# Thirteen accumulating transfers begun by GpSimd beside four pairs of gate and up units of a decoder layer

## The chip, the cores and the metric

The kernel runs on one core of a Trainium2 chip. A core has TensorE (matrix products), VectorE, ScalarE and GpSimd (called POOL in the profile), and SyncE (SP), whose queue begins most transfers; sixteen transfer engines move the bytes. Each engine works through its instructions in order. The metric is the time of one execution on the device in microseconds; smaller is better. A profiled execution has a span as well, from its first to its last instruction.

## The reference

One decoder layer on 2048 tokens of width 1024: a mixing block of two head groups (a gated linear recurrence, and sliding-window attention with sinks), an output projection, and a gated MLP with a causal convolution of three taps; then a normalisation. The change lies in the MLP, which is

```python
v = rmsnorm(h, norm_ffn_w[l])
gate = causal_depthwise_conv(v @ w_gate[l], conv_w[l], conv_b[l])
h = h + (jax.nn.silu(gate) * (v @ w_up[l])) @ w_down[l]
```

with D_FF = 2816 columns in w_gate and w_up.

## The kernel before, in words

Activations lie transposed: features on the 128 partitions, tokens along the row. The tokens are worked in two halves (hf = 0 and 1) of 1024. In each half come the mixing block, the output projection, the stage gate_up, and the stage down. All operands are fp32 split into a high and a low part, and each product of blocks is three matmuls.

gate_up loops over 11 pairs (pr = 0 to 10) of feature tiles, 2 x 128 columns of w_gate and of w_up. A pair is two units, one for gate and one for up. A unit is a 2 x 2 block product done with seven block products in place of eight (Winograd's form): on the weight side the blocks are A11, A12, A22 and the sums S1 to S4, on the token side B11, B21, B22 and T1 to T4. Its 84 matmuls of 512 columns go to three banks X, Z and Y; ScalarE copies the results s1, u2, s5 and u3 to a ring of seven tiles of 128 x 512 (tag "ut", UT = 7), and VectorE adds them up.

prep_pair loads the two weight tiles of the next unit (raw4 at L192, on SP's queue, into a ring of three raw tiles), forms S1 to S4 on VectorE (L934 to L937), and splits all operands: the high part is a cast on ScalarE (L800), the low part a subtraction on VectorE (L801).

After the gate unit follow convolution, SiLU and the normalising factor, which give two tiles y1 and y2 of 128 x 1024; the evacuation of the up unit multiplies its results into them (L1085), half by half. They come from a pool of eight tiles of 128 x 1024 (slot, tag "m"), which also holds S, Sh, Sl and S4 of the weights. At the end of a pair the seven token-side operands of the down stage are formed and stored to scratch in device memory:

```python
nc.sync.dma_start(dst["B11"], y1[:, lo])      # L1095; B21 and B22 from y2 follow
...
nc.vector.tensor_tensor(y1[:, lo], tt[:, hi], y1[:, lo], op=ALU.add)       # L1102
nc.sync.dma_start(dst["T2"], y1[:, lo])                                    # L1103
nc.vector.tensor_tensor(y2[:, lo], y2[:, lo], y1[:, lo], op=ALU.subtract)  # L1104
nc.sync.dma_start(dst["T4"], y2[:, lo])                                    # L1105
```

So the lower halves of y1 and y2 are overwritten in place, and whatever reads them must have read them before. These operands (act0B11, act0T4 and so on) are read again only in the down stage, whose products are written out in `product` and `prep_piece`.

The framework derives all waits from the reads and writes of tiles, and plans the order of each engine's instructions ahead of time with estimated times of its own (`schedule_with_timeline_sim=True`); the text's order is only a priority, except where `issue_after` pins it. GpSimd works in the head of the kernel and sets zeros in the mixing block; in gate_up it has nothing to do, and it begins no transfer anywhere.

Of the kernel before, what the change touches and what calls it, by code (L numbers as in the profile page):

```python
# [8 lines left out]
F32 = mybir.dt.float32  # L9
# [4 lines left out]
ALU = mybir.AluOpType  # L14
# [3 lines left out]
P = 128  # L18
D = 1024
# [21 lines left out]
UT = 7  # L41
# [12 lines left out]
def hymba_layer(ctx: ExitStack, tc: tile.TileContext, a: dict, out: bass.AP):  # L54
    nc = tc.nc

    def pool(name, bufs=1, space=None, stack=ctx, **kw):
        if space is not None:
            kw["space"] = space
        return stack.enter_context(tc.tile_pool(name=name, bufs=bufs, **kw))  # L60
# [7 lines left out]
    dp = pool("dram", space=bass.MemoryType.DRAM)  # L68
# [277 lines left out]
    def slot(name):  # L346
        return hp.tile([P, HALF], F32, tag="m", name=name, bufs=KT)
# [455 lines left out]
    @contextmanager  # L803
    def behind(*instructions):

        with ExitStack() as st:
            for i in instructions:
                st.enter_context(tc.issue_after(i.ins))
            yield
# [102 lines left out]
    def prep_pair(src1, src2, home=None, ut=None):  # L912

        r1, r2 = raw4(src1), raw4(src2)
        lo, hi = slice(0, 512), slice(512, D)

        def ring():
            return (wp.tile([P, D], F32R, tag="hi", name="whi", bufs=2),
                    wp.tile([P, D], F32R, tag="lo", name="wlo", bufs=2))

        def m(name, shape=[P, D], dt=F32R):
            return hp.tile(shape, dt, tag="m", name=name, bufs=KT)

        A = None if home else ring()
        if A:
            split_into(*A, r1)

        if home:
            S1, S2, S4 = [ut(n) for n in ("S1", "S2", "S4")]
        else:  # L930
            S = m("S", [P, D], F32)
            S1, S2, S4 = S[:, lo], S[:, hi], r1[:, hi]
        B = Sh, Sl = [(home or m)(n) for n in ("Sh", "Sl")]
        nc.vector.tensor_tensor(S1, r2[:, lo], r2[:, hi], op=ALU.add)  # L934
        nc.vector.tensor_tensor(S2, S1, r1[:, lo], op=ALU.subtract)
        nc.vector.tensor_tensor(r2[:, lo], r1[:, lo], r2[:, lo], op=ALU.subtract)
        nc.vector.tensor_tensor(S4, r1[:, hi], S2, op=ALU.subtract)  # L937
        if home:
            split_into(Sh[:, hi], Sl[:, hi], S2)
            split_into(Sh[:, lo], Sl[:, lo], S1)  # L940
        else:
            split_into(Sh, Sl, S)
        if not A:
            A = ring()
            split_into(*A, r1)
        R = ring()
        dd = m("S4", [P, 2, 512])

        def rest():
            split_into(*R, r2)  # L950
            split_into(dd[:, 0], dd[:, 1], S4)

        if not home:
            rest()
        cut = lambda t, c: (t[0][:, c], t[1][:, c])
        return {"A11": cut(A, lo), "A12": cut(A, hi), "S1": cut(B, lo), "S2": cut(B, hi),
                "S3": cut(R, lo), "A22": cut(R, hi), "S4": (dd[:, 0], dd[:, 1]), "rest": rest}
# [65 lines left out]
    def gate_up(hf, ops, hs, nxt, last, p):  # L1023

        acts = {op: [dp.tile([P, n, 512], F32, name=f"act{hf}{op}{i}") for i, n in enumerate(PIECES)] for op in OPS}
        lo, hi = slice(0, 512), slice(512, HALF)
        invb = hs.acc

        def ring(name, dt=F32):
            return p.tile([P, 512], dt, tag="ut", name=name, bufs=UT)  # L1030

        srcs = [w[2 * pr:2 * pr + 2] for pr in range(FT // 2) for w in (a["w_gate"], a["w_up"])]
        for pr in range(FT // 2):
            f0 = 2 * pr
            W, nxt = nxt, None

            ga = [p.tile([P, HALF + 64], F32, tag="ga", name="ga", bufs=2)[:, 0:2 + HALF] for _ in range(2)]

            def gate(i, j, x, y):
                dst = ga[i][:, 2 + j * 512:2 + (j + 1) * 512]  # L1040
                iv = invb[:, j * 512:(j + 1) * 512]
                if y is not None:
                    nc.vector.tensor_tensor(dst, x, y, op=ALU.add)
                    x = dst
                later.append(lambda: nc.vector.tensor_tensor(dst, x, iv, op=ALU.mult))
                if pr:
                    flush()

            def flush():
                while later:  # L1050
                    later.pop(0)()

            later = []
            then = {"S4": lambda: hs.everywhere(ring, ("mm", "mm"), True), "A22": flush} if pr == 0 else {}
            if pr == 0:
                def behind_first(copied):
                    nonlocal nxt
                    with behind(*last(copied)):
                        nxt = prep_pair(srcs[1][0], srcs[1][1])

                pair_unit(W, ops, p, gate, then, behind_first)
            else:
                nxt = prep_pair(srcs[2 * pr + 1][0], srcs[2 * pr + 1][1])
                pair_unit(W, ops, p, gate, then)
            flush()
            ys = []
            for i in range(2):
                ft, g = f0 + i, ga[i]
                nc.scalar.copy(g[:, 0:2], halo[:, ft])
                nc.scalar.copy(halo[:, ft], g[:, HALF:HALF + 2])  # L1070
                y = slot("y")
                nc.scalar.activation(y, g[:, 2:2 + HALF], AF.Identity, scale=C.cw[:, ft, 2:3], bias=C.cw[:, ft, 3:4])  # L1072
                for w in (1, 0):
                    nc.vector.scalar_tensor_tensor(y, g[:, w:w + HALF], C.cw[:, ft, w:w + 1], y,  # L1074
                                                   op0=ALU.mult, op1=ALU.add)
                nc.scalar.activation(y, y, AF.Silu)
                nc.vector.tensor_tensor(y, y, invb, op=ALU.mult)
                ys.append(y)

            def up(i, j, x, y):  # L1080
                dst = ys[i][:, j * 512:(j + 1) * 512]
                if y is not None:
                    nc.vector.tensor_tensor(y, x, y, op=ALU.add)
                    x = y
                nc.vector.tensor_tensor(dst, x, dst, op=ALU.mult)  # L1085

            W = nxt
            if pr + 1 < FT // 2:
                nxt = prep_pair(srcs[2 * pr + 2][0], srcs[2 * pr + 2][1])
            pair_unit(W, ops, p, up)  # L1090

            y1, y2 = ys
            dst = {op: acts[op][pr // 2][:, pr % 2] for op in OPS}
            tt = slot("T13")
            nc.sync.dma_start(dst["B11"], y1[:, lo])  # L1095
            nc.sync.dma_start(dst["B21"], y2[:, lo])
            nc.sync.dma_start(dst["B22"], y2[:, hi])
            nc.vector.tensor_tensor(tt[:, lo], y1[:, hi], y1[:, lo], op=ALU.subtract)
            nc.sync.dma_start(dst["T1"], tt[:, lo])
            nc.vector.tensor_tensor(tt[:, hi], y2[:, hi], y1[:, hi], op=ALU.subtract)  # L1100
            nc.sync.dma_start(dst["T3"], tt[:, hi])
# [4 lines that stand above are left out]
        return acts  # L1106
# [184 lines left out]
    for hf in range(NH):  # L1291
        X, kv, invb, rs, f0 = nxt
        with ExitStack() as st:
            p = pool(f"mix{hf}", stack=st, reuse_waits="tile")
# [7 lines left out]
            for n, step in enumerate(ORDER.split()):  # L1302
                i = int(step[1:] or 0)
# [16 lines left out]
        with ExitStack() as st:  # L1320
            p = pool(f"ffn{hf}", stack=st, reuse_waits="tile")
            kept, ops, hs, first, last = out_proj(hf, M, p)
            acts = gate_up(hf, ops, hs, first, last, p)
            nxt = down(hf, kept, acts, p)
# [61 lines left out]
```

## Time and profile before

| | |
|---|---|
| time, median of 2 runs | 2113.93 us (2113.62 to 2114.24) |
| span of the profiled execution | 2112.5 us |
| the profiled execution's own time | not listed apart from the runs; their median is 1.4 us above the span |
| TensorE matmul, busy | 2098.0 us (99%) |
| VectorE / ScalarE / GpSimd, busy | 1624.3 / 1088.1 / 24.6 us |
| SP's and ScalarE's hardware queues | 251.45 and 1.85 MB |
| mean granted clock of TensorE | 0.999 |

The page gives busy times by engine for the whole span, and shares of time of the chain of work that ended last; other views of the same trace give the instructions in order of time (start, duration, engine, line, operation, output and inputs, and in brackets the idle time before with what ended it), the waits summed by pairs of lines (total, number, longest), and busy times in chosen stretches. A busy TensorE counts overlapping matmuls once. "SPq" rows are SP's issues of transfers: their duration is that of the issue and not of the transfer.

### The profile page before, as it was taken

Reading aid. Unit: us, or ns where it says so; the run is one execution under the profiler, and the core shown is the slowest. Engines: PE = TensorE matmul, PEld = TensorE weight load, DVE = VectorE, ACT = ScalarE, POOL = GpSimd, SP = SyncE. Lnnn points to the kernel's source line nnn. Section 1 sums busy time; section 2 is a strip of 40 time slices with the busy share of each in tenths; the row PEclk is TensorE's granted clock in tenths of the full one; section 3 lists DMA queues with packets and bytes.
Section 4 is the critical chain, followed back from the end, with each engine's and each line's share of the span. In section 5 each row is a group of like instructions: output and inputs, shape, how many; then the busy total and the mean of one; then the engine's idle time right before and its main releaser. Section 6 shows DMA issues by size and latency. Waiting matters only on the chain.

```text
span 2112.5 us, 29613 instructions
## 1 busy us (share of the span) xinstructions
PE 2098.0 (99%) x11480; PEld 1740.9 (82%) x11480; DVE 1624.3 (77%) x2355; ACT 1088.1 (52%) x1877; POOL 24.6 (1%) x52
## 2 busy tenths in 40 slices
PE   9999999999999999999999999999999999999998
PEld 7888888888888888888888888888888888888887
DVE  7457887898888878786773677868988788887766
ACT  6365565664444445345744566656544444444354
POOL 2000000000000000000000000000000000000000
PEclk9999999999999999999999999999999999999999
DMA  4111111513332325964641111214233233269643
GB/s 161 42 51 34 33 42 53 175 60 115 102 122 86 119 96 185 389 213 157 218 134 52 31 34 35 77 45 149 80 100 130 88 102 120 85 217 385 230 149 135
DMA packets 96617, 255.19 MB, mean 121 GB/s; under 512 B 17370, under 2 KB 19802, under 8 KB 96476
## 3 DMA queue, kind: packets, MB, share of 16 engines
q1 hardware_dynamic: 91220, 251.45, 34.9%
q10 hardware_dynamic: 5256, 1.85, 0.3%
q8 instruction: 90, 1.47, 0.3%
q14 instruction: 51, 0.42, 0.1%
HBM read 195.11 MB, written 57.16 MB: 119 GB/s over the span
## 4 chain that ended last, share of the span: by engine, by line
PE 96%; ACT 2%; DMA 1%; DVE 1%; issue 0%; SPq 0%; DVEq 0%
PE X L975 8%; PE X L976 8%; PE X L977 8%; PE pop L222 7%; PE hq L222 4%; PE q L222 4%; PE f L222 4%; PE pdx L1193 4%; PE pdx L1194 4%; PE pdx L1195 4%; PE Y L977 4%; PE Y L976 4%; PE Y L975 4%; PE g L222 3%; PE pdy L1194 3%; PE pdy L1193 3%
## 5 line engine op out<-in xcount | busy, mean ns | idle before, releaser
L800 ACT CAST whi<-raw 128x1024 fp32r<-128x1024 f32 x88 | 92.6, 1052 | 110.0 <-PE X L976 74.1
L975 PE MATMUL X<-T,whi 128*128 128x512 f32 x352 | 137.4, 390 | 0.0
L976 PE MATMUL X<-T,whi 128*128 128x512 f32 x352 | 137.0, 389 | 0.0
L977 PE MATMUL X<-T,wlo 128*128 128x512 f32 x352 | 137.0, 389 | 0.0
L1074 DVE SCALAR_TENSOR_TENSOR y<-ga,cw,y 128x1024 f32<-128x1024 f32 x88 | 112.3, 1278 | 25.7 <-ACT y L1072 25.7
L201 DVE TENSOR_TENSOR wlo<-raw,whi 128x1024 fp32r<-128x1024 f32 x57 | 69.3, 1218 | 60.8 <-ACT whi L200 60.5
L982 ACT COPY u<-X 128x512 f32<-128x512 f32 x88 | 51.6, 587 | 121.4 <-PE X L977 121.3
L801 DVE TENSOR_TENSOR wlo<-raw,whi 128x1024 fp32r<-128x1024 f32 x88 | 107.1, 1217 | 2.1 <-ACT whi L800 2.1
L200 ACT CAST whi<-raw 128x1024 fp32r<-128x1024 f32 x57 | 59.6, 1048 | 77.9 <-PE q L222 22.3
L222 PE MATMUL pop<-XL,whi 128*128 128x512 f32 x256 | 88.8, 391 | 0.0
L222 PE MATMUL pop<-XH,whi 128*128 128x512 f32 x256 | 88.0, 393 | 0.0
L222 PE MATMUL pop<-XH,wlo 128*128 128x512 f32 x256 | 87.1, 390 | 0.0
L801 DVE TENSOR_TENSOR xld<-raw,xhd 128x1024 fp32r<-128x1024 f32 x72 | 80.2, 1129 | 8.7 <-ACT xhd L800 8.6
L679 ACT COPY G<-QK 128x1024 f32<-128x1024 f32 x48 | 51.4, 1071 | 66.7 <-DVE QK L683 45.5
L800 ACT CAST xhd<-raw 128x1024 fp32r<-128x1024 f32 x72 | 68.9, 978 | 27.0 <-DMA raw<-act1B 6.0
L975 PEld LDWEIGHTS X<-T,whi 128*128 128x128 f32 x352 | 66.0, 188 | 15.1 <-ACT u L982 1.6
L977 PEld LDWEIGHTS X<-T,wlo 128*128 128x128 f32 x352 | 66.1, 188 | 13.8
L976 PEld LDWEIGHTS X<-T,whi 128*128 128x128 f32 x352 | 66.1, 188 | 13.7
L683 DVE TENSOR_TENSOR QK<-QK,f 128x1024 f32<-128x1024 f32 x56 | 68.5, 1223 | 11.3 <-ACT G L679 11.1
L1194 PE MATMUL pdx<-xld,hid 128*128 128x512 f32 x192 | 74.7, 389 | 0.0
L1193 PE MATMUL pdx<-xhd,hid 128*128 128x512 f32 x192 | 74.2, 390 | 0.0
L1195 PE MATMUL pdx<-xhd,lod 128*128 128x512 f32 x192 | 72.4, 389 | 0.0
(393 smaller groups left out, 6280.6 us busy)
## 6 DMA issues: line engine op xcount, KB each, us to landing
wr<-in_w_down SPq DMA_DIRECT2D x90, 512.0 KB
raw<-in_w_gate SPq DMA_DIRECT2D x44, 512.0 KB
raw<-in_w_up SPq DMA_DIRECT2D x44, 512.0 KB
raw<-act0T SPq DMA_DIRECT2D x20, 512.0 KB
raw<-act1T SPq DMA_DIRECT2D x20, 512.0 KB
act0B<-y SPq DMA_DIRECT2D x33, 256.0 KB
act1B<-y SPq DMA_DIRECT2D x33, 256.0 KB
raw<-in_w_out SPq DMA_DIRECT2D x16, 512.0 KB
```

Source lines behind the costliest of these rows:

```text
L201: nc.vector.tensor_tensor(lo, raw, hi.bitcast(F32), op=ALU.subtract)
L222: marks["unit"] = nc.tensor.matmul(o[b], w, x[:, bs], start=f, stop=l)
L683: done = nc.vector.tensor_tensor(own, own, Fv.rearrange("p b w -> p w b").unsqueeze(3).to_broadcast([P, 2, nb, m]), op=ALU.mult)
L800: return (nc.scalar.copy(h, src), (eng or nc.vector).tensor_tensor(l, src, h.bitcast(F32), op=ALU.subtract))
L801: (eng or nc.vector).tensor_tensor(l, src, h.bitcast(F32), op=ALU.subtract))
L975: nc.tensor.matmul(o, wh[:, ws], xh, start=i == 0 and not more, stop=False, skip_group_check=more)
L976: nc.tensor.matmul(o, wh[:, ws], xl, start=False, stop=False, skip_group_check=more)
L977: r = nc.tensor.matmul(o, wl[:, ws], xh, start=False, stop=i == 3, skip_group_check=more)
L1074: nc.vector.scalar_tensor_tensor(y, g[:, w:w + HALF], C.cw[:, ft, w:w + 1], y, op0=ALU.mult, op1=ALU.add)
L1193: nc.tensor.matmul(o, wh[:, i, c], ah[:, i, cols], start=f, stop=False, skip_group_check=more)
L1194: nc.tensor.matmul(o, wh[:, i, c], al[:, i, cols], start=False, stop=False, skip_group_check=more)
L1195: nc.tensor.matmul(o, wl[:, i, c], ah[:, i, cols], start=False, stop=l, skip_group_check=more)
```

## The change

In half 0 two scratch tensors of 128 x 2048 in device memory are added, sums[0] and sums[1], which nothing outside the added lines reads. At the end of four pairs, ahead of the stores of the seven operands, `added` is called with y1 and y2:

- pr = 3: SP stores y1 and y2 to both tensors (four transfers of 512 KB).
- pr = 4: GpSimd begins six transfers that add to what lies at their destination: three of 256 KB from the lower half of y1 to three column ranges of sums[0], and three of 512 KB from y2 to sums[1], of which the first two have the same destination.
- pr = 5: GpSimd begins four adds from sums[1] to sums[0], two of 512 KB and two of 1 MB.
- pr = 6: SP loads 256 KB of sums[0] to a tile of the ring "ut", GpSimd begins three adds of 256 KB from sums[1] to this tile, and SP stores it back.

The store of descriptors that GpSimd's transfers use grows from 256 to 512 bytes per partition.

```diff
+        sums = [dp.tile([P, 2 * D], F32, name=f"sum{i}") for i in range(2)] if hf == 0 else None
+
+        def added(pr, y1, y2):
+
+            if pr == 3:
+                for i, t in enumerate(sums):
+                    nc.sync.dma_start(t[:, 0:D], y1)
+                    nc.sync.dma_start(t[:, D:2 * D], y2)
+            elif pr == 4:
+                for c in (slice(0, 512), slice(512, D), slice(D, D + 512)):
+                    nc.gpsimd.dma_start(sums[0][:, c], y1[:, 0:512], accum_op=ALU.add)
+                for c in (slice(0, D), slice(0, D), slice(D, 2 * D)):
+                    nc.gpsimd.dma_start(sums[1][:, c], y2, accum_op=ALU.add)
+            elif pr == 5:
+                for _ in range(2):
+                    nc.gpsimd.dma_start(sums[0][:, 0:D], sums[1][:, 0:D], accum_op=ALU.add)
+                for _ in range(2):
+                    nc.gpsimd.dma_start(sums[0], sums[1], accum_op=ALU.add, max_dma_last_dim=8192)
+            else:
+                t = p.tile([P, 512], F32, tag="ut", name="added", bufs=UT)
+                nc.sync.dma_start(t, sums[0][:, 0:512])
+                for i in range(3):
+                    nc.gpsimd.dma_start(t, sums[1][:, i * 512:(i + 1) * 512], accum_op=ALU.add)
+                nc.sync.dma_start(sums[0][:, 0:512], t)
...
             dst = {op: acts[op][pr // 2][:, pr % 2] for op in OPS}
+            if hf == 0 and pr in (3, 4, 5, 6):
+                added(pr, y1, y2)
             tt = slot("T13")
...
-    nc = bacc.Bacc("TRN2", target_bir_lowering=False, num_devices=1, dynamic_dma_scratch_size=256)
+    nc = bacc.Bacc("TRN2", target_bir_lowering=False, num_devices=1, dynamic_dma_scratch_size=512)
```

## The prediction

> **What bounds the kernel now.** I read the page's busy times first, then who waits for TensorE's operands, then the stage of the change.
>
> ```profile
> span 2112.5 us, 29613 instructions
> PE 2098.0 (99%) x11480; PEld 1740.9 (82%) x11480; DVE 1624.3 (77%) x2355; ACT 1088.1 (52%) x1877; POOL 24.6 (1%) x52
> q1 hardware_dynamic: 91220, 251.45, 34.9%
> ```
>
> Matmuls fill 2098.0 of 2112.5 us. All that is not matmul is 14.5 us, so no reordering can win more than 0.7%, and every stall that reaches TensorE is added to the time. GpSimd is nearly empty, and there is no software queue among the transfers: what a transfer begun by GpSimd costs, this trace doesn't show. The last row gives a price for plain bytes: 251.45 MB in 34.9% of 2112.5 us (737 us) is 341 GB/s while the transfer engines work, so 512 KB (0.524 MB) takes 1.54 us of them.
>
> The waits of TensorE, longest first, are these:
>
> ```profile
> PE psc L520 <- DVE sc L529: 2.6, 2, 1.3
> PE kv L420 <- ACT whi L363: 1.3, 1, 1.3
> PE idle L104 <- DVE ones L91: 1.1, 1, 1.1
> PE psum L308 <- DVE invb L256: 1.0, 1, 1.0
> PE psum L325 <- ACT fsq L262: 0.5, 1, 0.5
> ```
>
> None is in the gate and up stage. The change sits there, in half 0; these are its stretches, with busy time of TensorE, weight loads, VectorE, ScalarE and GpSimd, then clock, share of the transfer engines and GB/s:
>
> ```profile
> 570.00:606.00 36.00, 36.00 (x161) 29.80 (x160) 30.02 (x40) 15.68 (x23) 0.00 (x0) 1.00 0.34 108
> 606.00:643.00 37.00, 37.00 (x165) 30.65 (x164) 29.77 (x39) 16.27 (x23) 0.00 (x0) 1.00 0.31 100
> 680.00:717.00 37.00, 37.00 (x165) 30.62 (x164) 29.75 (x39) 14.97 (x23) 0.00 (x0) 1.00 0.31 107
> ```
>
> TensorE is full at clock 1.00. VectorE works 29.8 of 37 us, so it can make up some 7 us per pair; two thirds of the transfer engines' time are free, and GpSimd does nothing. So the change can only hurt through what is **queued behind it in order**: VectorE, which overwrites y1 and y2, and SP's queue.
>
> **The change, part by part.** Here are SP's issues and VectorE's instructions around the end of the pair pr = 4 (start, duration), the pair in which the first six adds are begun:
>
> ```profile
> 612.83 0.33 SPq L1095 DMA_DIRECT2D act0B<-y  x1
> 614.57 0.33 SPq L192 DMA_DIRECT2D raw<-in_w_up  x1
> 624.77 0.32 SPq L1103 DMA_DIRECT2D act0T<-y  x1
> 627.72 0.32 SPq L1105 DMA_DIRECT2D act0T<-y  x1
> ```
>
> ```profile
> 612.12 0.68 DVE L1085 TENSOR_TENSOR y<-s,y 128x512 f32<-128x512 f32 x1
> ...
> 622.86 0.68 DVE L934 TENSOR_TENSOR S<-raw 128x512 f32<-128x512 f32 x1
> 623.46 0.68 DVE L1085 TENSOR_TENSOR y<-X,y 128x512 f32<-128x512 f32 x1
> 624.06 0.68 DVE L1102 TENSOR_TENSOR y<-T,y 128x512 f32<-128x512 f32 x1
> ...
> 627.00 0.69 DVE L1104 TENSOR_TENSOR y<-y 128x512 f32<-128x512 f32 x1
> 627.61 1.22 DVE L801 TENSOR_TENSOR Sl<-S,Sh 128x1024 fp32r<-128x1024 f32 x1
> ```
>
> The lower half of y1 is ready at 612.80, y2 as a whole at 624.14. L1102 overwrites the lower half of y1 at 624.06, L1104 that of y2 at 627.00. Both now wait for the adds that read these bytes as well.
>
> *Price of one add.* Nothing in the trace shows it; I bound it by plain transfers. The latency of a landed transfer:
>
> ```profile
> DVE strip L654 <- DMA odd<-moved: 14.0, 15, 2.4
> ACT h L874 <- DMA keep<-h: 10.2, 11, 2.6
> ```
>
> Waits for 31 KB between partitions reach 2.4 us and those for a 256 KB store 2.6 us, so I take 2.5 us from begin to landing beside the bytes. From below, an add moves the bytes of a plain transfer: 1.54 us per 512 KB. An add must also read its destination, twice the bytes: I take 3.1 us per 512 KB, the nearest to the row. From above there is no row; I keep an add at eight times the plain price (12 us per 512 KB) as the far end. So an add of 256 KB takes 4.0 us, of 512 KB 5.6 us, of 1 MB 8.7 us. [...]
>
> *pr = 3: four stores on SP.* Four issues of 0.33 us make 1.3 us of SP's queue, and 2 MB take 4 x 1.54 = 6.2 us of the transfer engines, which are two thirds free here. They read y1 and y2, so the overwriting of pair 3 may slip by two stores' 3.1 us. Weights have cover: the load issued at 614.57 is first read at 622.86 by L934, 8.3 us. I take 0 (from 0 to 3).
>
> *pr = 4: six adds.* Three of 256 KB from y1 go to different columns; one after another they land at 612.80 + 3 x 4.0 = 624.8, against 624.06 for L1102: at most 0.7 us late, and none if they overlap. The three of 512 KB from y2 can't start before 624.14; the second adds to what the first added to, and waits, and the third is behind it in GpSimd's queue. They land at 624.14 + 3 x 5.6 = 640.9. L1104 thus comes 13.9 us later than at 627.00. Nothing needs its result, the store L1105, before the down stage, but two things are behind it. On VectorE these are the split of Sl at 627.61 and all the splits and sums that follow; on SP, the weight loads after L1105. The next readers on TensorE:
>
> ```profile
> 630.61 0.39 PE L977 MATMUL X<-B,wlo 128*128 128x512 f32 x1
> ...
> 641.03 0.39 PE L977 MATMUL X<-T,Sl 128*128 128x512 f32 x1
> ```
>
> The Sl split ends at 628.83 and is first read about 641.03, so 12.2 us of cover; were VectorE to stand 13.9 us at L1104, TensorE would lose 1.7 us there, and more at the next splits, since the lost time is made up at only 7 us per pair: 13.9 - 7 = 6.9 us at worst of the first pair. If the planner puts L1104 later among VectorE's instructions, the loss is 0. The rows speak for that: in the quoted stretch L934, which is the next unit's weight and later in the program's text, stands ahead of L1102, so this order follows readiness and not the text. I take 2 of 0 to 7 us.
>
> *pr = 5: four adds between scratch tensors*, 2 x 5.6 + 2 x 8.7 = 28.6 us, each behind the one before. No engine reads or writes these tensors until pair 6, and GpSimd has no other work until the next half. Pair 6 begins its stores and reaches its own y2 here:
>
> ```profile
> 688.99 0.33 SPq L1095 DMA_DIRECT2D act0B<-y  x1
> ...
> 699.62 0.68 DVE L1085 TENSOR_TENSOR y<-X,y 128x512 f32<-128x512 f32 x1
> ```
>
> Two pairs lie between 612.83 and 688.99, so a pair takes 38.1 us and a unit 19. If the four adds begin straight behind pair 4's, they end at 640.9 + 28.6 = 669.5; if only at the end of pair 5 (624.14 + 38.1 = 662.2), at 690.8. That leaves 9 to 30 us of cover. Six times 512 KB at 3.1 us are 18.6 us of the transfer engines, which shares them with weight loads: a load of 1.54 us becomes at worst 3.1, within the 8.3 us of cover. I take 0 (to 2).
>
> *pr = 6: a load into a ring tile on SP, three adds of 256 KB to it, one after another, and a store on SP.* 2.5 + 0.8 for the load, 3 x 4.0 for the adds, 4.0 for the store. If SP stands at the store from the load on, it stands for some 15 us; a weight load has 8.3 us of cover, so that 7 us would reach TensorE. If the store is put where its data are due, SP doesn't stand. The ring has seven tiles and a unit of 19 us takes four: one tile held 19 us leaves six for a demand of four. I take 1 (from 0 to 7).
>
> [...]
>
> *Scratch for descriptors*: 256 more bytes of each partition; no row prices an address, I take 0.
>
> The sum on the profiled execution is 2112.5 + 0 + 2 + 0 + 1 = 2115.5 us of span. The median of the runs, 2113.93, lies 1.4 us above that span, so 2117 us.
>
> **The rivals.**
>
> *VectorE or SP is held* (0.15): the planner leaves L1104, or SP's store of pair 6, where it would be if adds were quick, and the adds are two or three times dearer than my 3.1 us. At 7 us per 512 KB the chain from y2 takes 3 x (2.5 + 7) = 28.5 us, L1104 is 25.7 us late, and with 7 made up 18.7 are lost: 2114 + 19 = 2133. I give it 2124 to 2140. For it: the stage has no slack on TensorE, and one instruction in order holds all. Against it: the order of the rows follows readiness.
>
> *Adds that are truly slow* (0.07, slower than 2%; another 0.03 for its lower part, 2140 to 2156). With x us per 512 KB, pair 4's chain and pair 5's behind it end at 624.14 + 7 x 2.5 + 9x = 641.6 + 9x. SP reaches pair 6's load about 699.6 and stands there in order, with every weight load and activation store behind it; 8.3 us are covered. The loss is 9x - 66.3 us: nothing up to x = 7.4, and over 42 us (2%, about what a measurement of this kernel can tell from no change) from x = 12, where it gives 2156. That is 44 GB/s, an eighth of the plain rate. For it: no row shows an add. Against: the same engines, and rows of 2 to 8 KB each.
>
> *The transfers are not there* (0.03): nothing reads the scratch in the end; were they dropped, 2114 would stay.
>
> *A luckier order* (0.02): the planner re-plans everything behind pair 3, and some of the 14.5 us are saved: 2108 to 2112.
>
> **How the numbers follow.** My forecast, 2112 to 2124 around 2117, has 0.70: its open terms are 0 to 7, 0 to 3, 0 to 2 and 0 to 7 us, and not all at their ends. With the missing transfers it holds 0.73; so the range reaches over the first rival, to 2140, and leaves out 0.12. Faster by over 2% is impossible with 14.5 us to win; I leave 0.01. Slower by over 2% is the slow add, 0.07. The rest, 0.92, is within 2%.
>
> **What the profile after would show.** A software queue with thirteen transfers, some 6.3 MB of adds; GpSimd with thirteen issues between 612 and 715 us. L1104 of pair 4 about 640, with VectorE's idle time before it near zero if the planner moved it, and named as a wait for GpSimd's transfer if not. SP's wait before pair 6's load is to be nil, and TensorE full in all four pairs. The prediction is wrong if an add of 512 KB lands in more than 10 us, if a wait of VectorE for such an add is over 10 us, or if the planner's new order costs TensorE idle time far from the adds, in the down stage or in half 1.

## The result, and the profile after

The changed kernel takes 2129.82 us (median of 2 runs, 2129.35 to 2130.28) against 2113.93: the ratio is 1.0074 (95% interval 1.0045 to 1.0104), some 15.6 us. The time lies inside the predicted range, but not in its likeliest case, 2112 to 2124: it lies in that of the first rival, in which VectorE is held. The added lines move the overwriting of y1 from L1102 to L1129 and that of y2 from L1104 to L1131; the store of y2's lower half, L1096, is L1123 now, and the stores and adds of `added` lie from L1038 to L1055.

The page of the changed kernel, its span, busy times and transfer queues:

```profile
span 2127.6 us, 29635 instructions
PE 2100.7 (99%) x11480; PEld 1741.6 (82%) x11480; DVE 1624.1 (76%) x2355; ACT 1088.1 (51%) x1877; POOL 34.5 (2%) x65
q1 hardware_dynamic: 92084, 254.07, 34.5%
q0 software_dynamic: 1872, 6.29, 1.9%
```

The span grew by 15.1 us and the work of VectorE and ScalarE not at all. TensorE is busy 2.7 us longer, so its idle time grew by 12.4 us. The new software queue (packets, MB, share of sixteen engines) is the thirteen adds: 6.29 MB in 1.9% of 2127.6 us, some 40 us, hence about 156 GB/s. The plain bytes of the prediction ran at 341.

TensorE's longest waits in the changed kernel (total, times, longest):

```profile
PE Y L975 <- ACT Sh L800: 5.5, 1, 5.5
PE X L975 <- ACT s L982: 3.5, 1, 3.5
PE psc L520 <- DVE sc L529: 2.9, 2, 1.5
PE X L975 <- ACT u L982: 2.0, 2, 1.7
```

Three of the four are new and belong to the gate and up stage, which had none before. The stretches of the change, with the columns of the prediction's table, show in which pairs:

```profile
606.00:643.00 37.00, 31.51 (x133) 25.69 (x132) 22.33 (x29) 10.13 (x15) 4.57 (x5) 0.95 0.61 136
643.00:680.00 37.00, 32.40 (x140) 25.81 (x140) 28.21 (x36) 15.16 (x22) 4.26 (x5) 1.00 0.75 160
680.00:717.00 37.00, 35.33 (x157) 28.91 (x156) 28.46 (x37) 14.36 (x21) 2.71 (x3) 1.00 0.52 152
```

TensorE was full in the first and the last of these stretches; now it is idle for 5.5, 4.6 and 1.7 us, together 11.8 of the 12.4. In the first stretch the clock is 0.95, too. Now the cause, backwards from TensorE. First two rows of ScalarE, the cast of Sh, for which the 5.5 us wait is named, and a small copy ahead of that of s; then VectorE's instructions around the two overwritings (start, duration; in brackets the idle time before, and what ended it):

```profile
632.51 1.04 ACT L800 CAST Sh<-S 128x1024 fp32r<-128x1024 f32 x1 [9.74 <-DVE S L935]
...
651.18 0.19 ACT L1095 COPY halo<-ga 128x2 f32<-128x2 f32 x1 [12.09 <-DVE ga L1070]
```

```profile
622.33 1.22 DVE L801 TENSOR_TENSOR wlo<-raw,whi 128x1024 fp32r<-128x1024 f32 x1
631.18 0.69 DVE L1129 TENSOR_TENSOR y<-T,y 128x512 f32<-128x512 f32 x1 [7.63 <-DMA sum<-y]
631.79 0.69 DVE L935 TENSOR_TENSOR S<-S,raw 128x512 f32<-128x512 f32 x1
...
634.72 1.22 DVE L801 TENSOR_TENSOR Sl<-S,Sh 128x1024 fp32r<-128x1024 f32 x1
...
637.89 0.69 DVE L801 TENSOR_TENSOR S<-raw,S 128x512 fp32r<-128x512 f32 x1 [0.74 <-ACT S L800]
649.07 0.69 DVE L1131 TENSOR_TENSOR y<-y 128x512 f32<-128x512 f32 x1 [10.49 <-DMA sum<-y]
649.68 0.69 DVE L1068 TENSOR_TENSOR ga<-u,s 128x512 f32<-128x512 f32 x1
```

VectorE stands 7.63 us at L1129 for the adds that read y1. Directly behind it in the queue is L935, whose S ScalarE casts to the Sh that TensorE needs next: idle in turn are VectorE, ScalarE (9.74 us) and TensorE (5.49 us). After eight more instructions it stands 10.49 us at L1131 for the adds that read y2, with the evacuations of the gate unit (L1068, L1070) behind it; ScalarE stands 12.09 us at a copy of their result, its copy of s from the bank X is behind that, and TensorE waits 3.5 us for the bank. (The rest of this stretch's 4.6 us are two shorter waits further on, 0.8 and 0.3 us.) So the waits sit on VectorE, but why do the adds land so late? GpSimd's own instructions, those of pair 4 and the last of pair 5:

```profile
614.03 1.05 POOL L1042 DMA_DIRECT2D sum<-y  x1 [322.50 <-DVE y L1110]
619.59 0.90 POOL L1042 DMA_DIRECT2D sum<-y  x1 [4.50 <-issue]
626.40 0.87 POOL L1042 DMA_DIRECT2D sum<-y  x1 [5.91 <-DMA act0B<-y]
631.27 0.88 POOL L1044 DMA_DIRECT2D sum<-y  x1 [4.01 <-issue]
637.57 0.87 POOL L1044 DMA_DIRECT2D sum<-y  x1 [5.41 <-issue]
643.52 0.88 POOL L1044 DMA_DIRECT2D sum<-y  x1 [5.08 <-issue]
...
671.22 0.85 POOL L1049 DMA_DIRECT2D sum<-sum  x1 [7.93 <-DMA sum<-sum]
```

The three adds from y1 go to different columns and wait for nothing of each other, yet they begin 5 to 7 us apart, about the time in which one lands. "issue" means that GpSimd waited for nothing that the profile shows; for the third the view names a store of y, which this add does not need and behind which it does not stand in the first experiment. The row from y2 can begin only behind them, at 631.27, though y2 was ready at 620.23. That is the reading to be tested: the adds go one at a time, in a queue of GpSimd's own.

The third gap, 1.7 us, is of another kind. Here is the chain of work that ended last, cut to 620 to 700 us (start, duration), and then VectorE's row:

```profile
673.54 10.82 DMA act0B<-y
```

```profile
684.46 0.69 DVE L1131 TENSOR_TENSOR y<-y 128x512 f32<-128x512 f32 x1 [5.67 <-DMA act0B<-y]
```

It is pair 5's own store of y2's lower half, begun on SP at 673.54, that takes 10.82 us to land. Pair 5's second add of 1 MB was begun 2.3 us before it, and the two adds of 1 MB took 8.4 and 11.9 us to land. Meanwhile the transfer engines are full (next to last column, the share of them):

```profile
672.00:678.00 6.00, 6.00 (x28) 4.99 (x27) 6.00 (x10) 2.65 (x4) 0.07 (x1) 1.00 0.97 210
678.00:684.00 6.00, 6.00 (x29) 4.95 (x28) 0.79 (x1) 0.61 (x2) 0.00 (x0) 1.00 0.95 280
```

### The profile page after: what moved, and what is told of

Its sections match the earlier page's. It is cut to its first block, busy times and chain, and to the rows that moved or that the text cites. A ratio compares the mean times of both kernels' runs of the same rounds, so it can differ in the third digit from the quotient of the medians.

```text
span 2127.6 us, 29635 instructions
## 1 busy us (share of the span) xinstructions
PE 2100.7 (99%) x11480; PEld 1741.6 (82%) x11480; DVE 1624.1 (76%) x2355; ACT 1088.1 (51%) x1877; POOL 34.5 (2%) x65
## 3 DMA queue, kind: packets, MB, share of 16 engines
q0 software_dynamic: 1872, 6.29, 1.9%
## 4 chain that ended last, share of the span: by engine, by line
PE 66%; DVE 1%; DMA 1%; ACT 1%; issue 0%; DVEq 0%; ACTq 0%
PE X L975 5%; PE X L976 5%; PE X L977 5%; PE pdx L1220 4%; PE pdx L1222 4%; PE pdx L1221 4%; PE pop L222 4%; PE pdy L1222 3%; PE pdy L1220 3%; PE pdy L1221 3%; PE Y L977 3%; PE Y L976 3%; PE Y L975 3%; PE hq L222 2%; PE q L222 2%; PE f L222 2%
## 5 line engine op out<-in xcount | busy, mean ns | idle before, releaser
L975 PEld LDWEIGHTS X<-T,whi 128*128 128x128 f32 x352 | 66.3, 188 | 17.8 <-ACT u L982 4.2
L975 PE MATMUL Y<-T,Sh 128*128 128x512 f32 x176 | 68.9, 391 | 5.5 <-ACT Sh L800 5.5
```

The lines of the kernel that those rows point to most:

```text
L975: nc.tensor.matmul(o, wh[:, ws], xh, start=i == 0 and not more, stop=False, skip_group_check=more)
```

## Experiments

Each was timed against the kernel before, on the same chip; the ratios are to that kernel. The runs come from two chips, and the changed kernel has its first two runs only, so differences between experiments are taken from these ratios or, where so said, from medians. A, B and so on are the theories that the expectations name.

### A wider store of descriptors, the same work

```diff
-dynamic_dma_scratch_size=512
+dynamic_dma_scratch_size=2048
```

> The change as it is, with a descriptor store of 2048 instead of 512 bytes per partition; the order of every engine is the same. Theory A (GpSimd begins one add at a time because its store of descriptors holds only one, and VectorE stands at the overwriting of y1 and y2 behind the whole row of adds): the gaps of 4 to 6 us between GpSimd's first six issues shrink to about 1 us, the overwriting of y1 waits under 2 us instead of 7.6, that of y2 under 6 instead of 10.5, and the time is 2116 to 2123 us. Rival B (the adds themselves are the limit: the transfer engines work them off one after another anyway): the issues move together but the landings don't, and the time stays at 2127 to 2131 us.

Measured: 2117.55 us, 1.0014 (1.0005 to 1.0024). Every engine's instructions stand in the same order as in the changed kernel. GpSimd's begins with 2048 bytes:

```profile
614.06 2.85 POOL L1042 DMA_DIRECT2D sum<-y  x3 [322.21 <-DVE y L1110]
620.55 1.74 POOL L1044 DMA_DIRECT2D sum<-y  x2 [3.64 <-DVE y L1110]
629.07 0.86 POOL L1044 DMA_DIRECT2D sum<-y  x1 [6.78 <-DMA sum<-y]
```

The three adds from y1 begin back to back, and y2's row begins when y2 is ready, at 620.55 instead of 631.27. Each add of y1 takes longer to land, 8.7 us (median) against 5.3, but they are under way together. VectorE's waits in these pairs and TensorE's:

```profile
DVE y L1131 <- DMA act0B<-y: 4.6, 1, 4.6
...
DVE y L1131 <- DMA sum<-y: 1.6, 1, 1.6
```

```profile
PE X L975 <- ACT u L982: 1.6, 1, 1.6
```

L1129 waits no more, L1131 for 1.6 us instead of 10.49, and of TensorE's gaps only the third is left, but for 0.3 us. The bytes are the same and the adds more crowded (the transfer engines are busy 0.75 of the first stretch, against 0.61), so their traffic was not what cost these gaps. So some 12 of the 15.6 us hang on the size of this store. That it is the "issue" time that went is shown; that GpSimd stood for room in the store is inferred from this: with 2048 bytes three begins take 2.85 us, with 512 they take 13.2 us.

### Half of that store

```diff
-dynamic_dma_scratch_size=512
+dynamic_dma_scratch_size=1024
```

> The change as it is, with 1024 bytes per partition for descriptors instead of 512 (2048 gave 2117.55 us); same order on every engine. Theory A (one add's descriptors fill a store of 512 bytes so that the next must wait): a store twice as large holds two or three adds, GpSimd's second issue follows the first in about 1 us and a later one waits; VectorE's waits before the overwriting of y1 and y2 are shorter than at 512, and the time lies between, 2116 to 2122 us. Rival (the store mattered at 2048 through something else, such as where tiles lie): 2127 us or more.

Measured: 2117.68 us, 1.0014 (1.0005 to 1.0024), the same as with 2048; here, too, the first three begin back to back. Of y2's row the second add begins 3.3 us behind the first (621.16 and 624.42), while with 2048 bytes the two are back to back. The step that matters to the time lies between 512 and 1024 bytes.

### Plain transfers in place of adds

```diff
-nc.gpsimd.dma_start(sums[0][:, c], y1[:, 0:512], accum_op=ALU.add)
+nc.gpsimd.dma_start(sums[0][:, c], y1[:, 0:512])
```

and so at all five calls: the scratch tensors are overwritten and nothing is added.

> The thirteen transfers are plain copies instead of adds, in the same order on every engine (the scratch then holds other values; the output doesn't depend on it). Theory A: what counts is how long one transfer holds the store of descriptors; a plain one moves half the bytes, 256 KB lands in some 3 to 4 us instead of 5.3, 512 KB in 4 instead of 5.6, and the loss halves: 2119 to 2125 us. Rival C (a transfer begun by GpSimd costs a fixed 4 to 5 us whatever it does): the landings stay within 0.5 us of those of the adds and the time at 2127 to 2131 us.

Measured: 2114.28 us, 0.9998 (0.9989 to 1.0008), with the same orders on every engine. Nothing is lost, which is better than any theory expected. GpSimd's first begins, the software queue and the first stretch of this kernel:

```profile
613.08 1.80 POOL L1042 DMA_DIRECT2D sum<-y  x3 [322.01 <-DVE y L1110]
619.70 1.08 POOL L1044 DMA_DIRECT2D sum<-y  x2 [4.81 <-DVE y L1110]
```

```profile
q0 software_dynamic: 1488, 6.29, 0.8%
```

```profile
606.00:643.00 37.00, 37.00 (x165) 30.66 (x164) 30.43 (x40) 16.00 (x23) 5.01 (x9) 1.00 0.57 194
```

The same bytes take 0.8% of the span, 17 us of the engines, against 40. They also have 1488 packets against 1872, and 512 bytes of store are wide enough for them: three begin in 1.80 us. So this run changes two things at once, the price and the room.

### Plain transfers with a store half as wide

The same edit as above, and

```diff
-dynamic_dma_scratch_size=512
+dynamic_dma_scratch_size=256
```

> Plain copies in place of the adds, with a store of 256 bytes instead of 512; same order on every engine. It tells whether the narrow store alone, without the dearer adds, holds VectorE. Theory A: GpSimd's issues are then apart by a whole transfer again, some 4 us for 256 KB and 5 us for 512 KB; y1's row of three ends about 626, y2's about 641, and the time is 2116 to 2122 us, between the plain copies at 512 bytes (2114.28) and the adds (2129.82). Rival F (only the adds' own price counts): 2113 to 2115 us.

Measured: 2115.06 us, 1.0005 (0.9996 to 1.0014), under the range that I had set and at the edge of rival F's. The price stays low here and the room is taken away: GpSimd begins one at a time again, and VectorE waits again, which rival F does not have:

```profile
613.70 0.73 POOL L1042 DMA_DIRECT2D sum<-y  x1 [322.35 <-DVE y L1110]
616.93 0.54 POOL L1042 DMA_DIRECT2D sum<-y  x1 [2.50 <-issue]
```

```profile
DVE y L1129 <- DMA sum<-y: 3.4, 1, 3.4
DVE y L1131 <- DMA sum<-y: 2.7, 1, 2.7
```

But a plain transfer of 256 KB lands in 3.7 us (median) where an add takes 5.3, so that the waits are 3.4 and 2.7 us instead of 7.6 and 10.5, and TensorE loses 0.3 us. About 3 us of a stopped VectorE are covered here. One at a time is thus not enough by itself: the loss needs the narrow store and the dearer transfer together.

### Without the six adds of pair 4

```diff
-if hf == 0 and pr in (3, 4, 5, 6):
+if hf == 0 and pr in (3, 5, 6):
```

> The six adds of the second pair are left out; the stores of the first, the four adds between scratch tensors and the last pair's three stay. Theory A: 2114 to 2118 us, since those six cost nearly all. Rival D or a rival E (the new order of instructions costs time wherever it is): 2122 us or more.

Measured: 2115.27 us, 1.0003 (0.9994 to 1.0012); TensorE has no wait from 560 to 760 us. The order of the rest is planned anew in this kernel, and pair 5's two adds of 1 MB begin early, at 605.32 and 614.15.

### The six adds with another source

```diff
-nc.gpsimd.dma_start(sums[0][:, c], y1[:, 0:512], accum_op=ALU.add)
+nc.gpsimd.dma_start(sums[0][:, c], sums[1][:, 0:512], accum_op=ALU.add)
-nc.gpsimd.dma_start(sums[1][:, c], y2, accum_op=ALU.add)
+nc.gpsimd.dma_start(sums[1][:, c], sums[0][:, 0:D], accum_op=ALU.add)
```

All thirteen adds stay, with their bytes, but pair 4's read scratch and hold neither y1 nor y2.

> The six adds of the second pair read the other scratch tensor instead of y1 and y2 (same sizes and number, still one at a time); so nothing of the stage waits for them and no tile of the ring of eight is held, while their bytes on the transfer engines stay or grow. TensorE's order is that of the change. Theory A (what costs is that y1 and y2 are held): TensorE is full in that pair, 2114 to 2118 us. Rival D (bytes on the transfer engines): 2122 us or more.

Measured: 2115.53 us, 1.0005 (0.9996 to 1.0015). No instruction of VectorE waits for an add, and TensorE is full in pair 4, though GpSimd still begins them one at a time. So what was lost hung on this, that the adds read tiles which VectorE is to overwrite. Two things differ besides: pair 4's adds no longer need y1 and begin 28 us earlier, at 585.57, and VectorE's order changes by a few places. In pair 5 the trace has a wait of TensorE that I had not expected:

```profile
PE Y L975 <- ACT Sh L800: 1.8, 1, 1.8
```

At L934 VectorE waits for weight loads here, 9.5 us in three waits between 560 and 760 us, the longest 5.5 us; in the changed kernel it is 3.3 us in two, the longest 1.8 us. That such a load is behind TensorE's wait is inferred from this. The two halves of this edit, one by one:

### Only y1 is held

The second of the two edits alone.

> Of the second pair's six adds only the three of 512 KB read the other scratch tensor instead of y2; the three of 256 KB still read y1 (five runs of VectorE's order change by a few places, TensorE's not). VectorE then waits once, some 7.6 us at the overwriting of y1, and not at that of y2. If the two waits add up, TensorE keeps the first gap of 5.5 us with its slow clock behind it and loses the second of 4.6 us: 2122 to 2126 us. If what counts is the sum of the waits beyond one cover, one wait of 7.6 us costs some 3 us less than its length: 2119 to 2122 us.

Measured: 2123.18 us, 1.0041 (1.0026 to 1.0056). VectorE's wait and TensorE's:

```profile
DVE y L1129 <- DMA sum<-y: 7.6, 1, 7.6
```

```profile
PE Y L975 <- ACT Sh L800: 5.6, 1, 5.6
```

### Only y2 is held

The first of the two edits alone.

> The reverse: the three adds of 256 KB read the other scratch tensor, those of 512 KB still read y2, now from about 620 us on and one at a time, so that they end about 638 us instead of 649. VectorE waits once, at the overwriting of y2, some 6 to 8 us. If the waits add up, one gap of 3 to 5 us of TensorE is left: 2118 to 2122 us; if y1's wait alone did the harm, 2115 to 2117 us.

Measured: 2120.64 us, 1.0028 (1.0018 to 1.0039).

```profile
DVE y L1131 <- DMA sum<-y: 10.4, 1, 10.4
```

```profile
PE X L975 <- ACT s L982: 1.9, 1, 1.9
```

Each wait of the changed kernel appears alone and at its length; I had expected 6 to 8 us for the second. The first has the gap that it had, the second a gap of 1.9 us instead of 3.5, behind which the clock is at half for some 3.4 us (see the last section). Beyond the kernel that holds neither (1.0005) they cost 0.36% and 0.23%, 7.6 and 4.9 us by the medians. The longer wait costs less. In the changed kernel 7.63 us of VectorE's standing became 5.49 us of gap, and 10.49 us became 3.48: what is behind L1131 is needed later than what is behind L1129.

### The six adds behind the overwritings

`added` of pair 4 is called behind L1132, the store T4; what the adds read of the lower halves are then the overwritten values.

```diff
-            if hf == 0 and pr in (3, 4, 5, 6):
+            if hf == 0 and pr in (3, 5, 6):
...
+            if hf == 0 and pr == 4:
+                added(pr, y1, y2)
```

> The six adds of the second pair are called behind the last overwriting of y2 instead of ahead of it, so they read the overwritten halves (the scratch holds other values) and no instruction of VectorE waits for them. Theory A: VectorE's waits for these adds vanish and TensorE is full in that pair; what is left is the 2 us of the pair after, so 2114 to 2118 us. Rival D (the adds' bytes on the transfer engines delay weight loads, which costs TensorE its time): TensorE's gaps stay, 2124 to 2130 us.

Measured: 2120.65 us, 1.0029 (1.0017 to 1.0040). Both theories missed it. Neither L1129 nor L1131 of pair 4 waits for an add, but:

```profile
DVE Sl L801 <- DMA sum<-y: 8.1, 1, 8.1
```

```profile
PE Y L975 <- ACT Sh L800: 5.3, 1, 5.3
```

The pool of eight tiles that holds y1 and y2 also holds the weights' S, Sh and Sl. The split of Sl needs a slot that an add from y still reads. The wait moved from an overwriting of the data to the next use of their memory.

### Without pair 5's four adds

```diff
-if hf == 0 and pr in (3, 4, 5, 6):
+if hf == 0 and pr in (3, 4, 6):
```

> The four adds between scratch tensors of the third pair are left out, the rest is the change. Theory A with its second part (the last gap of TensorE, 1.7 us, comes from activation stores that land late beside the two adds of 1 MB): that gap vanishes and the rest stays, 2126 to 2129 us. Rival: no difference, 2129 to 2131 us, if that gap is a late effect of the second pair.

Measured: 2127.77 us, 1.0063 (1.0048 to 1.0078). The last of the three stretches in this kernel:

```profile
680.00:717.00 37.00, 37.00 (x165) 30.61 (x165) 31.86 (x41) 16.48 (x24) 2.65 (x3) 1.00 0.49 142
```

The third gap is gone; the waits at L1129 and L1131 stay, with 8.1 and 10.5 us. By the medians the gap is worth 2 us; the two ratios' intervals overlap, so that the trace carries this point and not the times alone. The gap does not always come with these adds: the runs with only y1 held, with only y2 held and with the six adds behind the overwritings keep them, L1131 waits up to 5.0 us there for such a store, and TensorE loses 0.3 us at most.

### The wide store, and without pair 5's adds

The edits of the first experiment and of the last.

> A descriptor store of 2048 bytes and no adds in the third pair: the two causes that the runs so far name are both gone, while nine of the thirteen adds stay. If they are all, 2113 to 2116 us, no difference from the kernel before; if the re-planned order costs something by itself, 2117 us or more.

Measured: 2115.54 us, 1.0004 (0.9994 to 1.0013), 2.0 us less than with pair 5's adds, with intervals that overlap. TensorE waits for nothing from 560 to 760 us. With these two taken out, the change can't be told from none.

## Why the prediction was right and wrong

**What bounds the kernel:** right. The loss is 12.4 us of TensorE's idle time and 2.7 us of longer busy time, part of it the lower clock behind a gap, and it came through what is queued in order behind a wait.

**Price of one add:** right for 512 KB (5.6 us from begin to landing, median, as estimated), too low for 256 KB (5.3 against 4.0) and for 1 MB (10.1 against 8.7). That 512 KB came out is in part luck, since half the bytes take nearly as long and my sum has them 1.6 us apart. The assumption that an add costs twice a plain transfer came close: 40 against 17 us of the engines in all, a ratio of 2.4. The profile counts 6.29 MB for either, so no row shows the reading of the destination from which I had taken the factor of two.

**pr = 3, four stores:** 0 as predicted; the kernel with pairs 3, 5 and 6 alone is at 1.0003.

**pr = 4, six adds:** this step failed. I took 2 of 0 to 7 us. The two holds cost 7.6 and 4.9 us by the runs with one source each; in the changed kernel's trace they are two gaps of 5.5 and 4.6 us, and the low clock behind the first. With pair 5's 2 us that is 14.5 of the 15.6 us; the rest is within the intervals. Three parts of this step failed.

The first is y1's row of adds, "at most 0.7 us late". I had put the three one after another at 4.0 us each, 12 us in all. One after another they were, but they took 17.2 us, from 614.03 to 631.18: an add of 256 KB lands in 5.3 us, not 4.0, and GpSimd begins each only about when the one before has landed, 5.6, 6.8 and 4.9 us apart. (The overlap that I had allowed for came only with the wider store.) They thus release y1 at 631.18, not at 624.8. That delays y2 as well: its row, which takes 17.8 us where I had 16.8, begins at 631.27, not at 624.14, and lets L1131 go at 649.07, 8.2 us later than the 640.9 I had worked out. (With the wide store it begins at 620.55: in the new order y2 was ready sooner than I had taken over from the old one.) I had seen that the store of descriptors was doubled, and priced its address only, not its room.

The second is what stands behind L1102. I had worked out the cover of the Sl split behind L1104, 12.2 us, and passed over L935, although the profile before has it directly behind L1102:

```profile
624.66 0.68 DVE L935 TENSOR_TENSOR S<-S,raw 128x512 f32<-128x512 f32 x1
...
625.38 1.05 ACT L800 CAST Sh<-S 128x1024 fp32r<-128x1024 f32 x1 [1.44 <-DVE S L935]
...
627.43 0.39 PE L975 MATMUL Y<-T,Sh 128*128 128x512 f32 x1
```

This Sh is ready at 626.43 and read at 627.43, a cover of 1.0 us. The 0.7 us that I allowed would have fitted in; 7.63 us of wait became 5.49 us of gap.

The third is "If the planner puts L1104 later among VectorE's instructions, the loss is 0." It did: three instructions stand between the two overwritings in the old order, eight in the new one, the split of Sl among them. The loss was not 0, since L1131 now held what came behind it there, the evacuations of the gate unit. The order is the same whether the transfers are adds or plain, so the planner gave the adds no more time than plain transfers; that it took them for quick is inferred from this.

**pr = 5:** 0 of 0 to 2; measured 2 us, the far end. I had asked whether weight loads come late beside the 1 MB adds. What came late was an activation store that y2's overwriting waits for, 10.82 us from begin to landing. Where pair 4's adds read scratch it was, as inferred above, a weight load after all, despite the 8.3 us of cover that I had counted: VectorE waited up to 5.5 us for one, and TensorE lost 1.8 us.

**pr = 6:** 1 of 0 to 7; it costs nothing that a run shows. With the wide store and without pair 5 it is still there, at 1.0004.

**GpSimd's stalls:** with the wider store, at the same order of VectorE's instructions, pair 4's first three begins take 2.85 us in place of 13.2, so what VectorE ran meanwhile was not what held GpSimd here.

**The rivals:** the first, that VectorE is held, names the right engine and the right wait, and the time lies in its range, but not by its sum. It had adds two or three times dearer than 3.1 us per 512 KB, and one overwriting, that of y2, 25.7 us late at its old place. Measured are adds of 512 KB at the price that I had assumed, two waits of 7.63 and 10.49 us, and the dearer gap at y1's overwriting, which no rival has. That its range holds the time is in part luck. One of the signs that I had named for being wrong, a wait of VectorE over 10 us for such an add, is there with 10.49: the time lies in the range, the account of the likeliest case was wrong.

## To carry to other kernels

Before a transfer begun by GpSimd is priced by its bytes, look at how many of them its store of descriptors lets it have in flight: with 512 bytes an add began 4.9 to 6.8 us behind the one before it, about its landing of 5.3 us; with 2048 bytes three began in 2.85 us. Then ask of each tile that a transfer reads when its bytes and its memory are next written, by whom, and what stands directly behind that writer in its queue: here it was this neighbour's reader that paid, and 7.63 us of wait at y1's overwriting, with L935 directly behind it, became 5.49 us of idle TensorE. A wider store was worth 12 us here at an unchanged order of instructions.

## What the runs showed of the hardware

- An accumulating transfer moves its bytes at about 156 GB/s of the engines' busy time and a plain one begun by GpSimd at about 370 (6.29 MB in 1.9% and in 0.8% of the spans, both rounded; the plain ones take 0.9%, which makes 331, with the store of 256 bytes).
- A store of 256 KB on SP's queue took 10.82 us to land beside an add of 1 MB, with the transfer engines busy for 0.97 and 0.95 of the time (changed kernel, 672 to 684 us).
- TensorE's clock fell around some short gaps. Behind the gap of 5.49 us in the changed kernel (columns as above) it is at half, 6 matmuls in 2 us where the kernel before has 10 or 11:

```profile
634.00:636.00 2.00, 2.00 (x6) 1.52 (x6) 2.00 (x3) 0.52 (x2) 0.00 (x0) 0.50 1.06 245
```

With only y2 held, it fell around the end of a gap of 1.9 us (640.57 to 642.49):

```profile
644.00:646.00 2.00, 2.00 (x6) 1.52 (x6) 1.61 (x2) 1.30 (x2) 0.00 (x0) 0.50 0.52 102
```

In both runs it is at half for some 3.4 us, from about 633.2 and from about 642.8 on, worked out from the granted clock of the neighbouring stretches of 2 us (0.80 and 0.85 in the changed kernel, 0.69 and 0.96 with only y2 held). With the six adds behind the overwritings it is at half for some 6.8 us, from about 667.9 on, around a gap of 5.3 us. In the changed kernel it stayed at 1.00 behind the gaps of 3.5 and 1.7 us. So the length of the gap alone does not decide here. What does stays open, as does how many adds exactly a store of a given size holds.
